# First loads in places of their own, and a wider margin behind TensorE's deferrable matmuls, in a planned hybrid-attention step

## Chip, core and metric

The kernel runs on one core of one Trainium2 chip. The metric is the device time of one execution in microseconds (us). The engines are TensorE (PE; its weight loads, PEld, run beside its matmuls), VectorE (DVE), ScalarE (ACT), GpSimd (POOL) and SyncE (SP), which issues the DMA transfers. TensorE's clock has two levels here, 2.4 and 1.2 GHz, and the profile gives the granted one as a share of the upper.

## What is computed

One layer of a streaming encoder, for 512 prompt rows and 32 sample rows of width 1024:

```python
z = _rmsnorm(x, g) @ w_in
qa, ka, va, ga, qb, kb, vb, gb, qm, gm, qi, ki, wi = _split_cols(z)
...
oa = _band_prompt(qa, ka, va, rel_bias_a[l])      # 6 heads: chunk band with a learned bias
ob = _dsa_prompt(qb, kb, vb, qi, ki, wi)          # 6 heads: keys chosen by an index score
om = _attend(qm, mk, mv, None)                    # 4 heads: 256 memory rows
xp = _merge(xp, oa, ob, om, ga, gb, gm, w_out)    # x + concat(o * silu(gate)) @ w_out
```

The sample rows do the same against caches of 1024 (or 512) past rows. For the second group an indexer of 8 heads by 32 scores every admissible key, `relu(qi . ki)` weighted by `wi`, and each query attends only to its best 128 (prompt) or 256 (sample) keys. The memory's keys and values are `_rmsnorm(mem) @ w_mem_kv`. Outputs are both results and the new cache rows.

## The kernel before

All 545 rows' projections are matmuls in three terms (high by high, low by high, high by low part), since TensorE takes rounded fp32 operands: `wh` and `wl` are the high and low part of a weight tile, `xTh` and `xTl` those of the transposed rows (tokens and samples beside each other, 544 columns). The order of the work is: the index projection, the keys' and values' projections (`ka`, `va`), memory keys and values (`mk`, `mv`), queries and gates (`EARLY`), then the second group (`LATE`), then the output projection. Attention, the index scores and the choice of keys are woven in between.

**The planner.** No order is written out by hand. The class `Line` (from L44) reckons a clock for every engine while the program is built: `cost` (L62) prices an instruction, `lag` (L87) the way from one engine to another, `had` (L121) says when a tile will be ready, `op` (L140) advances the clocks. The projections are the main thread (`run`, L204). Everything else is a task, a generator that yields the time at which it wants to go on; the tasks stand in a heap, and before every projection matmul `beside` (L191) runs the tasks that are due by then. Each engine gets its instructions in the order in which they are written, and takes them in that order on the chip. So a task's time decides how many projection matmuls stand in front of its own ones. That time is mostly `line.at(tiles)`, the reckoned readiness plus `margin`, 0.3 us (L169). `room` (L292) waits until the planner reckons a PSUM bank to be free.

**The weights.** `w_list` names all weight tiles in their order of use. `w_load` (L409) issues their loads into four buffers `raw` on SyncE's queue; a load waits until the tile four before it has been split and, where the sample rows use it too, used. `w_split` (L418) rounds `raw` to `wh` on ScalarE and subtracts to `wl` on GpSimd. `w_sample` (L445) multiplies the 32 sample rows with the unsplit `raw` (operand `xF`, eight matmuls a party, two for each `raw`; the trace has sixteen entries for the eight), and then itself moves the bank to SBUF on ScalarE, adds the four parts and scales them on VectorE. Parties are the index, the first and the second group's natural-order projections; the first four `raw` after the index's are the keys' (`ka`), the next four the values' (`va`).

**The first loads.** `START` (L36) is the order of the first loads: `x` is a part of the transposed rows, `w` a weight tile, `t` the rotary tables, `r` a tile of natural rows for the norms, `m` a half of the transposed memory. `rows_load` (L590) puts the prompt's and sample's rows into two alternating buffers `nat`, so a load waits for the norm of the rows two before; the memory's rows lie in the places of `rank` and `gate0`. `norms` (L604) squares and sums a tile of rows on ScalarE, and GpSimd makes its factor `rs`; `spread` (L618) turns `rs` into rows by TensorE. The memory norm's gain `g_mem` is loaded last in this run; `mTh`, the memory's high part, is made with it on ScalarE.

**The deferrable matmuls.** `index_prompt` (L798) and `index_sample` (L843) score keys by the index; `KSs` holds the sample's past index keys, of which VectorE subtracts the rounded part. `picks` finds the thresholds: for the sample by 22 tests, each of them `passed` (L936): ScalarE counts (`okf`, in the trace `bf_ok`), TensorE sums the counts in one matmul, VectorE sets the next threshold, so each test waits for the one before. `sample` (L1109) and `attend` (L1443) are the attention: scores, softmax (`z`, its sums `st`), transposes of `z` by `ident` into `pt`, and `pt` times values. `turned_pair` (L1279) transposes a head pair of `ka`.

Helpers record every operation on one line, so all rows of the trace show L233; the operand names tell them apart.

Of the kernel before, what the change touches and what calls it, by code (L numbers as in the profile page):

```python
# [9 lines left out]
F32 = mybir.dt.float32  # L10
# [3 lines left out]
ALU = mybir.AluOpType  # L14
# [3 lines left out]
P = 128  # L18
# [17 lines left out]
START = "wxwxwxwtwwrrrrwwrmmrr"  # L36
# [7 lines left out]
class Line:  # L44
# [41 lines left out]
    @staticmethod  # L86
    def lag(of, to):  # L87

        if of == to or of is None:
            return 0.127 if to == "DVE" else 0.09 if to == "POOL" else 0.0  # L90
        return 0.95 if of == "SP" else 0.26 if to == "PE" else 0.2 if of == "PE" else 0.06 if of == "POOL" else 0.15
# [77 lines left out]
    def at(self, *tiles):  # L169
        return max(self.had(x) for x in tiles) + self.margin  # L170

# [91 lines left out]
def hybrid_step(ctx: ExitStack, tc: tile.TileContext, a: dict):  # L263
# [28 lines left out]
    def room(k=1):  # L292

        yield from line.wait(lambda: len(free_banks) >= k)
        while True:
            t = sorted(pp.free(f"b{b}") for b in free_banks)[k - 1]
            if t <= line.now():
                return
            yield t
            yield from line.wait(lambda: len(free_banks) >= k)  # L300
# [10 lines left out]
    ka = cp.tile([P, NT, 384], F32, tag="ka", name="ka")  # L311
    va = cp.tile([P, NT, 384], F32, tag="va", name="va")
# [6 lines left out]
    ysS = cp.tile([P, PAST + T], F32, name="ysS")  # L319
# [89 lines left out]
    def w_load():  # L409
        party = {p + j for _, p, _ in parties for j in range(NK // 2)}  # L410
        for i, (w, k, nk, lo, hi) in enumerate(w_list):
            yield from line.wait(lambda: allowed[0] > i and len(split) > i - 4 and (i - 4 not in party or i - 4 in met))
            yield wp.free("raw")
            raw = wp.tile([P, nk, hi - lo], F32, tag="raw", name="raw", bufs=4)
            DMA.dma_start(raw, w[k * P:(k + nk) * P, lo:hi].rearrange("(k p) n -> p k n", p=P))
            raws.append(raw)
# [28 lines left out]
    def w_sample():  # L445
        for nm, i, n in parties:
            yield from line.wait(lambda: len(raws) > i + 1 and x_done[0] > 1)
            yield line.at(xF[:, 0:4, :], raws[i + 1])
            yield from room()
            p = bank()  # L450
            for j in (0, 2):
                yield from line.wait(lambda: len(raws) > i + j + 1 and x_done[0] > j + 1)
                yield line.at(raws[i + j], raws[i + j + 1], xF[:, 2 * j:2 * j + 4, :])
# [4 lines left out]
            yield line.at(p)  # L458
            if nm in ("kb", "vb"):
                yield from line.wait(lambda: 0 in over)  # L460
            out = (cp.tile([T, 384], F32, tag={"kb": "kaS", "vb": "vaS"}.get(nm, nm + "S"), name=nm + "S") if nm != "i"
                   else ix.tile([T, n], F32, name="zS"))
            A.copy(out, p[0:T, 0:n])
            for q in range(1, 4):
                yield line.at(out) - 0.2
                V.tensor_tensor(out, p[q * T:(q + 1) * T, 0:n], out, op=ALU.add)
            give(p)
            yield from line.wait(lambda: NT in normed)
            yield max(line.at(rs[0:T, NT:NT + 1]), line.at(out) - 0.2)
            V.tensor_scalar(out, out, rs[0:T, NT:NT + 1], None, op0=ALU.mult)  # L470
            news[nm] = out
            if nm in ("kb", "qb"):
                rope(out.rearrange("p (h d) -> p h d", d=64), out, T, 6, 64, ctab["cos64S"], ctab["sin64S"], V)
# [116 lines left out]
    def rows_load():  # L590
# [5 lines left out]
        if i <= NT:  # L596
            yield from line.wait(lambda: len(normed) > i - 2)
            t = rp.tile([P, D], F32, tag="nat", name="nat", bufs=2)
        else:
            t = cp.tile([P, D], F32, tag=("rank", "gate0")[i - NT - 1], name="nat")  # L600
# [17 lines left out]
    def spread():  # L618

        yield from line.wait(lambda: NT in normed)  # L620
        yield line.at(rs)
# [130 lines left out]
    def index():  # L752
        nonlocal ip, identR
        yield from line.wait(lambda: len(indexed) == NT and NT in normed)
        p1.close()
        ip = pool(ipx, "ip", "right")
        identR = ip.tile([P, P], F32R, name="identR")
        V.tensor_copy(identR, ident)
        for g in (index_sample(), index_prompt(), picks()):
            line.spawn(g)  # L760
        load_tables(64)
# [36 lines left out]
    def index_prompt():  # L798
# [5 lines left out]
        yield line.at(kst)  # L804
# [7 lines left out]
        for t in range(1, NT):  # L812
            n = P * (t + 1)
            yield line.at(qst[t])
# [11 lines left out]
            yield line.at(QS)  # L826
# [16 lines left out]
    def index_sample():  # L843
# [14 lines left out]
        yield line.at(qsS)  # L858
# [14 lines left out]
        yield line.at(kst2)  # L873
# [5 lines left out]
        for k0, n in ((0, 512), (512, 512), (1024, T)):  # L879
            yield line.at(KSs)  # L880
# [7 lines left out]
            yield line.at(*rs)  # L888
# [33 lines left out]
    def sample_choice():  # L922
# [13 lines left out]
        def passed(of, bias, least_, scale=1.0):  # L936
# [4 lines left out]
            yield line.at(okf) - 0.2  # L941
# [137 lines left out]
    natural = {"ka": ka, "va": va}  # L1079

    def projections(order):
        for nm in order:
# [17 lines left out]
            else:  # L1100
                if nm not in natural:

                    line.until(lambda: (2 if nm == "kb" else 0) in over)
                    natural[nm] = cp.tile([P, NT, 384], F32, tag=nm, name=nm)
                of = f"new_{nm[1]}_{nm[0]}"
# [3 lines left out]
    def sample(mix, nh, nb, kt, cv, qT, kn, vn, pts, zin):  # L1109
# [6 lines left out]
        if kn is not None:  # L1116
            yield line.at(kn)
# [7 lines left out]
        yield line.at(qT, *kt)  # L1125
        yield from room(3)
        o_ps = bank()
        for g0 in range(0, nh, 4):
# [35 lines left out]
            yield line.at(z)  # L1164
# [18 lines left out]
            yield line.at(*(x[0] for x in blocks))  # L1183
            yield line.at(*cv)
# [94 lines left out]
    def turned_pair(nat, hp, then):  # L1279

        w = nat.shape[1] * P
        yield line.at(nat[:, :, hp * P:(hp + 1) * P])
# [55 lines left out]
    class Masked:  # L1338
# [57 lines left out]
        def turn(self):  # L1396
            pts = []
            for e in range(2):
                yield from line.wait(lambda: places[self.w] > 0)
                places[self.w] -= 1  # L1400
                yield line.at(self.z[e])
# [41 lines left out]
    def attend(i):  # L1443
# [9 lines left out]
        yield line.at(*pair.q, *pair.k)  # L1453
# [12 lines left out]
        yield line.at(*pts)  # L1466
# [220 lines left out]
```

## Time and profile before

| | us |
|---|---|
| median of 3 runs | 384.17 |
| lowest, highest run | 383.58, 387.33 |
| the profiled execution | 385.51 |
| its span (first to last recorded instruction) | 383.7 |

The mean granted TensorE clock of the profiled execution is 0.984 of full speed. All rows come from that one execution, which took 1.34 us longer than the median; its span leaves 1.8 us of it before the first and behind the last instruction. A matmul's busy time in the rows is what it took at the granted clock, so a stretch at the lower clock looks busy and does half as much.

### The profile page before, as it was taken

What the parts mean: (1) busy time and instruction counts of PE and PEld (TensorE: products, weight loads), DVE (VectorE), ACT (ScalarE), POOL (GpSimd) and SP (SyncE); (2) the same over time, 40 slices, a digit from 0 to 9 for tenths busy, and PEclk for the clock granted to TensorE, in tenths of its full rate; (3) what the DMA queues carried; (4) which work ended last, traced back from release to release, by engine and by line L of the source; (5) the groups of instructions that cost most, each with busy time, mean ns of one, the idle gap of its engine ahead of it and who ended that gap; (6) DMA issues with size and microseconds to landing.
All of it is one profiled execution on the core that took longest, in us unless ns stands there. A gap on an engine that the chain in (4) does not pass through costs nothing.

```text
span 383.7 us, 7976 instructions
## 1 busy us (share of the span) xinstructions
PE 362.8 (95%) x2961; PEld 324.6 (85%) x2961; DVE 286.1 (75%) x721; ACT 224.5 (59%) x529; POOL 186.1 (49%) x199
## 2 busy tenths in 40 slices
PE   8997889999999999999898999799999999999992
PEld 8795768999989888898697888799999877999992
DVE  3664877988999999999999997787755587422453
ACT  5664946898677777756475674323654556411353
POOL 1778862377433665416668623735224310633552
PEclk9999989999999999999998999989999999999998
DMA  7969641156564422112401220522145940230005
GB/s 248 309 209 290 194 140 58 61 172 186 166 205 141 124 72 57 42 42 80 114 24 61 85 63 27 164 56 55 43 156 195 370 167 2 78 140 4 0 15 219
DMA packets 41478, 46.35 MB, mean 121 GB/s; under 512 B 5184, under 2 KB 36544, under 8 KB 41440
## 3 DMA queue, kind: packets, MB, share of 16 engines
q1 hardware_dynamic: 41440, 45.85, 38.0%
q8 instruction: 23, 0.38, 0.4%
q14 instruction: 15, 0.12, 0.1%
HBM read 39.67 MB, written 6.16 MB: 119 GB/s over the span
## 4 chain that ended last, share of the span: by engine, by line
PE 67%; DVE 21%; DMA 5%; ACT 3%; issue 2%; SPq 1%; POOL 1%; POOLq 0%; DVEq 0%; ACTq 0%
PE bank L233 67%; DVE ysel L233 3%; DVE m L233 2%; DMA g_mem<-in_norm_mem_g_dram 2%; DVE z L233 2%; DMA raw<-in_w_in_dram 2%; DVE rank L233 1%; DVE st L233 1%; DVE rt L233 1%; DVE qbS L233 1%; SPq L233 1%; DMA cbi<-in_cache_b_kidx_dram 1%; DVE kbS L233 1%; ACT sq L233 1%; DVE rot L233 1%
## 5 line engine op out<-in xcount | busy, mean ns | idle before, releaser
L233 POOL TENSOR_TENSOR wl<-raw,wh 128x512 fp32r<-128x512 f32 (+2 forms) x68 | 107.7, 1592 | 116.0 <-ACT wh L233 105.6
L233 ACT ACTIVATE wh<-raw 128x512 fp32r<-128x512 f32 (+2 forms) x70 | 49.5, 715 | 43.4 <-PE bank L233 18.1
L233 PE MATMUL bank<-wh,xTh 128*128 128x384 f32 (+1 forms) x192 | 67.9, 354 | 0.0
L233 PE MATMUL bank<-wl,xTh 128*128 128x384 f32 (+1 forms) x192 | 64.9, 338 | 1.8 <-POOL wl L233 1.7
L233 PE MATMUL bank<-wh,xTl 128*128 128x384 f32 (+1 forms) x192 | 64.7, 337 | 0.0
L233 ACT ACTIVATE z<-z,st 128x256 f32<-128x256 f32 (+3 forms) x73 | 39.0, 548 | 23.9 <-DVE st L233 23.9
L233 PE MATMUL bank<-xTh,wh 128*128 128x272 f32 x208 | 46.5, 304 | 0.4 <-DVE st L233 0.4
L233 PEld LDWEIGHTS bank<-wh,xTh 128*128 128x128 f32 x192 | 37.3, 194 | 7.4 <-issue 6.5
L233 PE MATMUL bank<-xTl,wh 128*128 128x272 f32 x208 | 43.0, 288 | 0.0
L233 PE MATMUL bank<-xTh,wl 128*128 128x272 f32 x208 | 42.9, 288 | 0.0
L233 PEld LDWEIGHTS bank<-wl,xTh 128*128 128x128 f32 x192 | 37.2, 194 | 2.6 <-POOL wl L233 2.2
L233 PEld LDWEIGHTS bank<-wh,xTl 128*128 128x128 f32 x192 | 37.3, 194 | 0.4 <-DVE xTl L233 0.3
L233 PEld LDWEIGHTS bank<-xTh,wh 128*128 128x128 f32 x208 | 32.6, 189 | 3.1 <-issue 1.8
L233 PEld LDWEIGHTS bank<-xTl,wh 128*128 128x128 f32 x208 | 32.6, 188 | 0.0
L233 PEld LDWEIGHTS bank<-xTh,wl 128*128 128x128 f32 x208 | 32.6, 189 | 0.0
L233 PE MATMUL bank<-ident,z 128*128 128x128 f32 (+1 forms) x161 | 26.0, 281 | 1.7 <-ACT pt L233 1.1
L233 DVE TENSOR_TENSOR xr<-bank,xr 128x256 f32<-128x256 f32 (+1 forms) x24 | 12.3, 512 | 19.8 <-PE bank L233 19.7
L233 DVE MAX8 m<-ysel 128x8 f32<-128x256 f32 (+2 forms) x48 | 26.3, 548 | 0.0
L233 DVE MATCH_REPLACE8 ysel<-m,ysel 128x256 f32<-128x256 f32 (+2 forms) x48 | 26.0, 543 | 0.0
L233 PEld LDWEIGHTS bank<-ident,z 128*128 128x128 f32 (+1 forms) x161 | 18.0, 142 | 5.8 <-issue 2.1
L233 ACT ACTIVATE junkS<-ysS,bi_neg 128x1056 int8<-128x1056 f32 x16 | 18.8, 1177 | 3.6 <-DVE bi_neg L233 3.6
L233 ACT COPY pt<-bank 128x512 f32<-128x512 f32 (+1 forms) x28 | 14.8, 539 | 8.8 <-PE bank L233 8.7
(308 smaller groups left out, 902.2 us busy)
## 6 DMA issues: line engine op xcount, KB each, us to landing
raw<-in_w_in_dram SPq DMA_DIRECT2D x20, 384.0 KB, 3.5
raw<-in_w_in_dram SPq DMA_DIRECT2D x26, 256.0 KB, 2.9
raw<-in_w_out_dram SPq DMA_DIRECT2D x8, 384.0 KB, 3.2
nat<-in_x_prompt_dram SPq DMA_DIRECT2D x4, 512.0 KB, 5.3
raw<-in_w_mem_kv_dram SPq DMA_DIRECT2D x8, 256.0 KB, 2.8
xr<-in_x_prompt_dram SPq DMA_DIRECT2D x4, 512.0 KB, 5.6
out_dram<-xr SPq DMA_DIRECT2D x4, 512.0 KB, 2.6
xr<-in_x_t_dram SPq DMA_DIRECT2D x3, 544.0 KB, 6.1
```

Of the source, the lines that this page charges most:

```text
L233: return fn(*args, **kw)
```

## The change

`START` puts all four keys' weights ahead of the rows, the four prompt and one sample row tiles behind them, and the memory rows behind the transposed memory. The first four of these `raw` tiles get places of their own (those of `q0` and `gate0`, which are written later), the next four then take the `raw` buffers, and none of the eight waits for a split. The rows 2 to 4 and the memory's get places of their own too (`ka`, `va`, `ysS`, `rank`, `gate0`), so that only the memory's wait, until the keys' samples are done with their weights. For that `ka`, `va` and `ysS` are allocated later. What follows the sample matmuls is a task of its own, `sample_rows`.

A new `Line.sure` reckons 1.0 us (`SURE`) behind the data instead of 0.3, and 20 places with a deferrable matmul use it instead of `at`; the choice's test, which took 0.2 off `at`, does too. `room` counts a bank as free 0.4 us later, and `lag` adds 0.3 us from a released place to TensorE.

```diff
-START = "wxwxwxwtwwrrrrwwrmmrr"
+START = "wxwxwxwtwwwwrrrrrmmrr"
+SURE = 1.0
...
+        if of is None and to == "PE":
+            return 0.3
         if of == to or of is None:
...
+    def sure(self, *tiles):
+
+        return max(self.had(x) for x in tiles) + SURE
...
-            t = sorted(pp.free(f"b{b}") for b in free_banks)[k - 1]
+            t = sorted(pp.free(f"b{b}") for b in free_banks)[k - 1] + 0.4
...
-    ka = cp.tile([P, NT, 384], F32, tag="ka", name="ka")
-    va = cp.tile([P, NT, 384], F32, tag="va", name="va")
+    ka = va = ysS = None
...
-            yield from line.wait(lambda: allowed[0] > i and len(split) > i - 4 and (i - 4 not in party or i - 4 in met))
-            yield wp.free("raw")
-            raw = wp.tile([P, nk, hi - lo], F32, tag="raw", name="raw", bufs=4)
+            yield from line.wait(lambda: allowed[0] > i and (i < 8 or len(split) > i - 4 and (i - 4 not in party or i - 4 in met)))
+            if i < 4:
+
+                if i % 2 == 0:
+                    first = cp.tile([P, 2, nk, hi - lo], F32, tag=("q0", "gate0")[i // 2], name="raw")
+                raw = first[:, i % 2]
+            else:
+                yield wp.free("raw")
+                raw = wp.tile([P, nk, hi - lo], F32, tag="raw", name="raw", bufs=4)
...
-                yield line.at(raws[i + j], raws[i + j + 1], xF[:, 2 * j:2 * j + 4, :])
+                yield line.sure(raws[i + j], raws[i + j + 1], xF[:, 2 * j:2 * j + 4, :])
...
+            line.spawn(sample_rows(nm, n, p))
+
+    def sample_rows(nm, n, p):
+        yield line.at(p)
...
-        if i <= NT:
-            yield from line.wait(lambda: len(normed) > i - 2)
+        if i < 2:
             t = rp.tile([P, D], F32, tag="nat", name="nat", bufs=2)
         else:
-            t = cp.tile([P, D], F32, tag=("rank", "gate0")[i - NT - 1], name="nat")
+            if i > NT + 1:
+                yield from line.wait(lambda: all(i in met for i in range(4)))
+            t = cp.tile([P, D], F32, tag=("ka", "va", "ysS", "rank", "gate0")[i - 2], name="nat")
...
-        yield from line.wait(lambda: len(indexed) == NT and NT in normed)
+        yield from line.wait(lambda: len(indexed) == NT and NT in normed and all(i in met for i in range(4)))
...
             for k0, n in ((0, 512), (512, 512), (1024, T)):
-            yield line.at(KSs)
+            yield line.sure(KSs)
             yield from room(2)
...
-            yield line.at(okf) - 0.2
+            yield line.sure(okf)
             yield from room()
...
-            yield line.at(z)
+            yield line.sure(z)
...
-                    line.until(lambda: (2 if nm == "kb" else 0) in over)
+                    line.until(lambda: NT - 1 in normed if nm[1] == "a" else (2 if nm == "kb" else 0) in over)
```

The first place is SyncE's queue behind the rotary tables, in the kernel before. `raw` 128x2x384 are the keys' and then the values' weights, `nat` natural rows, `mr` the transposed memory.

```order
L233 DMA raw<-in_w_in_dram 128x2x384 x2
L233 DMA nat<-in_x_prompt_dram 128x1024 x4
L233 DMA raw<-in_w_in_dram 128x2x384 x2
L233 DMA nat<-in_x_sample_dram 32x1024
L233 DMA mr<-in_mem_t_dram 128x4x256 x2
L233 DMA nat<-in_mem_prompt_dram 128x1024 x2
L233 DMA g_mem<-in_norm_mem_g_dram 128x8
```

The same place now:

```order
L240 DMA raw<-in_w_in_dram 128x2x384 x4
L240 DMA nat<-in_x_prompt_dram 128x1024 x4
L240 DMA nat<-in_x_sample_dram 32x1024
L240 DMA mr<-in_mem_t_dram 128x4x256 x2
L240 DMA nat<-in_mem_prompt_dram 128x1024 x2
L240 DMA g_mem<-in_norm_mem_g_dram 128x8
L240 DMA raw<-in_w_in_dram 128x2x384 x4
```

The third and fourth keys' weights moved ahead of four row tiles; the values' four weights, which stood seven issues further down, now follow the gain directly.

The second place is ScalarE after the first two index weights `wI` of the prompt, in the kernel before. `junk,ss` is a norm's square sum, `wh` a split.

```order
L233 ACTIVATE junk,ss<-nat 128x1024 x2
L233 ACTIVATE wh<-raw 128x768
L233 ACTIVATE junk,ss<-nat 32x1024
L233 ACTIVATE wh<-raw 128x768
L233 ACTIVATE stk<-rot 128x4x64
```

The same place now:

```order
L240 ACTIVATE junk,ss<-nat 128x1024 x2
L240 ACTIVATE mTh<-mr,g_mem 128x256
L240 ACTIVATE wh<-raw 128x768
L240 ACTIVATE junk,ss<-nat 32x1024
L240 ACTIVATE wh<-raw 128x768
```

A piece of the memory's high part moved ahead of the last keys' split and the sample's norm; the splits of the second and third keys' weights are no longer among these norms.

The third place is TensorE at the end of the index projection, now. `raw,xF` 32x384 are the keys' sample matmuls, which stood behind this projection, among the keys' own.

```order
L240 MATMUL bank<-wh,xTh_83 128x32
L240 MATMUL bank<-wh,xTl_85 128x32
L240 MATMUL bank<-wl,xTh_83 128x32
L240 MATMUL bank<-raw,xF 32x296 x4
L240 MATMUL bank<-raw,xF 32x384 x8
L240 MATMUL bank<-wh,xTh_83 128x296
L240 MATMUL bank<-wh,xTl_85 128x296
L240 MATMUL bank<-wl,xTh_83 128x296
```

The eight matmuls moved ahead of the projection's last quarter, so TensorE needs all four keys' weights before it.

The fourth place is TensorE in an attention piece over the memory, in the kernel before. `ident,z` transposes the softmax's `z`, `pt,mv` multiplies what came of it with the memory's values, `bf_ok,over` is a test of the choice.

```order
L233 MATMUL bank<-ident,z 128x128 x4
L233 LDWEIGHTS over_364
L233 MATMUL bank<-bf_ok,over_364 128x1
L233 MATMUL bank<-ident,mk 128x128 x2
L233 MATMUL bank<-ident,z 128x128 x4
L233 MATMUL bank<-pt,mv 64x128 x8
```

The same piece now, from the last of eighteen projection matmuls that follow `ident,mk`:

```order
L240 MATMUL bank<-wl,xTh_82 128x384
L240 MATMUL bank<-ident,z 128x128 x4
L240 MATMUL bank<-wh,xTh_82 128x384
L240 MATMUL bank<-wh,xTl_84 128x384
L240 MATMUL bank<-wl,xTh_82 128x384
L240 MATMUL bank<-wh,xTh_82 128x384
L240 MATMUL bank<-wh,xTl_84 128x384
L240 MATMUL bank<-wl,xTh_82 128x384
L240 MATMUL bank<-pt,mv 64x128 x8
```

Eighteen projection matmuls stand between the transposes of `mk` and those of `z`, and six between these and the product with the values, where none stood.

## Rows read from the trace of the kernel before

**Rows 1.** The page: busy us of each engine, share of the span, instructions.
```profile
PE 362.8 (95%) x2961; PEld 324.6 (85%) x2961; DVE 286.1 (75%) x721; ACT 224.5 (59%) x529; POOL 186.1 (49%) x199
```

**Rows 2.** Stretches: us, busy us (instructions) of PE, PEld, DVE, ACT, POOL, clock, DMA share, GB/s.
```profile
50.30:53.80 3.50, 3.50 (x16) 3.06 (x18) 3.47 (x4) 1.90 (x4) 3.25 (x4) 0.51 0.62 225
203.30:206.80 3.50, 3.04 (x22) 2.71 (x23) 3.37 (x9) 0.77 (x3) 3.05 (x4) 0.59 0.13 48
247.90:251.40 3.50, 3.36 (x12) 3.36 (x12) 3.09 (x4) 0.82 (x2) 2.21 (x1) 0.56 0.02 7
22.37:31.40 9.03, 9.03 (x52) 8.74 (x51) 4.63 (x14) 4.40 (x10) 7.43 (x20) 1.00 0.93 281
31.40:62.00 30.60, 26.14 (x161) 19.90 (x160) 21.53 (x35) 19.72 (x45) 20.24 (x30) 0.94 0.60 185
170.00:230.00 60.00, 55.96 (x459) 47.80 (x457) 57.63 (x131) 38.05 (x101) 35.90 (x32) 0.97 0.24 67
230.00:250.00 20.00, 17.61 (x121) 15.71 (x121) 15.43 (x29) 8.14 (x15) 11.30 (x9) 0.96 0.30 95
```

**Rows 3.** TensorE's waits, longest: matmul, releaser, total us, times, longest.
```profile
PE bank L233 <- ACT bf_ok L233: 2.4, 1, 2.4
...
PE bank L233 <- ACT z L233: 1.3, 1, 1.3
...
PE bank L233 <- DVE KSs L233: 1.1, 1, 1.1
...
PE bank L233 <- ACT pt L233: 1.1, 1, 1.1
...
PE bank L233 <- DVE pt L233: 0.8, 1, 0.8
...
PE bank L233 <- DVE ka L233: 0.7, 1, 0.7
```

**Rows 4.** Timeline of SyncE's queue: start, us on the queue, the DMA issued.
```profile
13.06 0.88 SPq L233 DMA_DIRECT2D raw<-in_w_in_dram  x2
13.99 9.52 SPq L233 DMA_DIRECT2D nat<-in_x_prompt_dram  x4
23.61 0.89 SPq L233 DMA_DIRECT2D raw<-in_w_in_dram  x2
```

**Rows 5.** DMA rate, 0 to 45 us in 40 slices of 1.125 us, from 0.
```profile
GB/s 0 11 273 303 322 318 294 390 380 387 350 153 63 337 378 386 405 62 22 0 211 288 255 378 381 252 211 312 353 403 408 311 216 150 204 69 136 395 388 393
```

**Rows 6.** Timeline of TensorE's matmuls: start, us, operation, in brackets idle us before, releaser.
```profile
32.56 0.45 PE L233 MATMUL bank<-wl,xTh 128*128 128x384 f32 x1 [1.12 <-POOL wl L233]
...
35.05 0.24 PE L233 MATMUL bank<-ident,rs 32*128 32x32 f32 x1 [1.08 <-POOL rs L233]
...
35.22 1.50 PE L233 MATMUL bank<-raw,xF 128*32 128x384 f32 x16
...
48.41 0.47 PE L233 MATMUL bank<-KSs,QSs 128*128 128x512 f32 x1 [1.14 <-DVE KSs L233]
```

**Rows 7.** Timeline of ScalarE, 31 to 33 us, columns as before.
```profile
31.14 1.06 ACT L233 ACTIVATE junk<-nat 32x1024 bf16<-32x1024 f32 x1 [1.84 <-DMA nat<-in_x_sample_dram]
32.20 0.83 ACT L233 ACTIVATE wh<-raw 128x768 fp32r<-128x768 f32 x1
```

**Rows 8.** Timelines of VectorE and of GpSimd from 45.3 us, columns as before.
```profile
45.46 2.80 DVE L233 TENSOR_TENSOR KSs<-cbi,KSs 64x1024 fp32r<-64x1024 f32 x1
...
45.34 1.84 POOL L233 TENSOR_TENSOR wl<-raw,wh 128x768 fp32r<-128x768 f32 x1 [1.02 <-ACT wh L233]
```

**Rows 9.** Views of tiles: count, ns (shortest, median, longest), first and last start, shapes.
```profile
L233 PE MATMUL bank<-bf_ok,over x22: 163/177/181, 69.3 to 248.0; 128*128 128x1 bf16 x22
...
L233 PE MATMUL bank<-keysB,qbS x36: 189/589/613, 306.7 to 323.0; 64*32 64x512 f32 x24, 64*32 64x32 f32 x12
...
L233 PEld LDWEIGHTS bank<-wh,oBh x48: 187/187/192, 357.6 to 375.6; 128*128 128x128 f32 x48
...
L233 ACT ACTIVATE oBh<-o x9: 292/311/420, 298.2 to 333.3; 128x128 fp32r<-128x128 f32 x6, 128x256 fp32r<-128x256 f32 x3
```

## Prediction made before the changed kernel was run

> **What bounds the kernel now.** I read the busy times first: TensorE is busy 362.8 us of a span of 383.7, so the time is TensorE's work plus the holes in it [rows 1]. Next the stretches: the holes lie in three places. From 31.40 to 62 us 4.46 us of 30.60 are idle, from 170 to 230 us 4.04 of 60, from 230 to 250 us 2.39 of 20 [rows 2]; together 10.9. The rest of the 20.9 idle us is the start, the tail behind the last matmul, and 1 us in small pieces. Third, the granted clock: 0.51, 0.59 and 0.56 over three stretches of 3.5 us [rows 2]. Each is a stretch at the lower level of 1.2 GHz, and what it costs is at most half of the busy time in it: about 1.7, 1.5 and 1.6, together 4.8. Fourth, TensorE's waits: the holes have names, each once: bf_ok 2.4, z 1.3, KSs 1.1, two of pt 1.1 and 0.8, ka 0.7 [rows 3], and in front wl 1.12 and rs 1.08 [rows 6]. TensorE takes its matmuls in the written order, so in each of these the matmul at the head was not ready while projection matmuls behind it were. No change of order can return more than 10.9 + 4.8 = 15.7 us.
>
> **The first loads.** The third and fourth of the keys' weights were behind four row loads, and these stood 9.52 us on SyncE's queue, because two of them wait for places [rows 4]. While SyncE waited the DMA engines ran dry: the rate falls to 63 GB/s at slice 12 and to 22 and 0 at slices 18 and 19 [rows 5]. That is why wl came 1.12 us late, and the sample's rows, which reached ScalarE at 31.14 [rows 7], made rs 1.08 late. Now nothing in that run of the queue waits for a place except the last memory rows, so both waits go: **-2.2 us**.
>
> What is late next? All loads now stand in one stream, and I time it by its bytes. It starts at 14.6 us, where slice 13 begins and the rate of the old kernel comes back. A full stream runs at 376 GB/s, the mean of slices 7 to 10 and of 13 to 16 alike; the mean of slices 20 to 33, with its gaps, is 295 [rows 5]. These are my two ends.
> - The keys' four weights, 1536 KB, have landed at 18.8 (19.9 at the low rate). The eight keys' sample matmuls, 1.50 us of work [rows 6], now stand ahead of the last quarter of the index projection. That quarter is 24 matmuls of 0.174 us at most (9.03 us for 52 [rows 2]) before 22.37, so TensorE comes to the last of these loads near 19: 0 to 0.9 us late.
> - The keys' projection then starts at 22.37 + 1.50 = 23.9. 66 of its matmuls at 0.174 bring TensorE to 35.4, where the first values' sample matmuls stand. Their second load is the 7524th KB of the stream: 35.1, or 40.7 at the low rate. Late by 0 to 5.3 us.
> - The memory norm's gain, a load of 4 KB, lies behind 5760 KB: 30.3 to 34.6. ScalarE now has mTh, which needs it, ahead of the fourth weights' split and of the sample's norm; so those two queue behind a load. In the old kernel 3.9 us passed from the sample rows' arrival, 31.14 [rows 7], to TensorE's release at 35.05 [rows 6]; with a split of 0.83 [rows 7] and mTh at as much again in front, TensorE is released at 35.9, or 40.2. It comes there at 35.4 + 0.75 (four sample matmuls) + 1.05 (six of the projection) = 37.2 at the earliest. Late by 0 to 3.0, and this hides behind the wait of the point above.
> - The rows are passed by 768 KB of weights but no longer wait for places: the first lands at 20.2, the fourth at 24.4, the sample's at 24.7, against 31.14 before. On ScalarE and GpSimd three splits of keys' weights now stand ahead of the first norm; nobody wants a norm before 37, so this costs nothing, nor does it that rows lie in the tiles of keys and values, which are first written after the keys' projection.
> I take 0.6 for all of it, near the fast end, since the full slices on both sides of each gap agree on 376; the ends are 0 and 5.3.
>
> **The margin.** A deferrable matmul was put 0.3 us behind its data as the planner reckons it, and is now put 1.0 behind; a bank's release 0 and now 0.4, with 0.3 more before TensorE is reckoned to start on it; the choice's test went from 0.1 to 1.0. Nothing is slept on the chip: the margin only sets how many projection matmuls stand in front. So each old wait shrinks by the added margin, at most to nothing: bf_ok 2.4 - 0.9 = 1.5, z 1.3 - 0.7 = 0.6, KSs 0.4, pt 0.7 (a bank) and 0.1, ka 0.3 (a bank). Of 7.4 remain 3.6: **-3.8 us**, with ends of 0 (as many waits at other places) and -7.4. At the memory units the order shows it: six projection matmuls now stand between z's transposes and pt's matmuls, where there were none.
>
> What else queues behind a later matmul? The longest serial chain is the sample's choice, 22 tests [rows 9]. At 0.9 us more each it ends 20 us later by plan, so its last test moves from 248.0 to about 268; the sample's scores begin at 306.7 [rows 9], so it stays hidden. At the end, the last attention piece leaves ScalarE at 333.3 and is first used at 357.6 [rows 9]; the new order has 152 matmuls behind its last attention piece, the old 213, so 24 us of cover become about 17. Both cost nothing.
>
> **The clock.** The falls came behind the largest holes: KSs, whose wait ends at 48.41 [rows 6], and ka right behind it, together 1.8; the two of pt, 1.9; bf_ok, 2.4. If the largest left is 1.5, I expect one fall of the three to stay: 4.8 - 1.6 = **-3.2 us**, with ends of 0 and -4.8.
>
> **Given back.** TensorE reaches the stage from 170 to 230 us some 4 us sooner, and there VectorE is busy 57.63 of 60 us [rows 2]: what it makes can hardly come sooner. The new order answers with more projection in front, but not everywhere: **+1.2**, ends 0 and 5.
>
> One measured pair bears on this. VectorE's subtraction of KSs took 2.80 us while GpSimd's wl ran from 45.34 for 1.84 [rows 8]; it ended 1.1 us after wl did, and that is what made TensorE wait 1.14. The Trainium skill has a rule for it (SBUF — State Buffer, section Who interferes with whom): GpSimd and VectorE share one pair of ports under an exclusive lock, and a VectorE instruction with two SBUF inputs waits out a GpSimd instruction that reads SBUF. The pair agrees with it. By that rule a margin of 1.0 does not cover a whole wl, and three such hits would leave 0.84 each, 2.5 us more, so that the sum would be 2.5 smaller; by the rows alone I count one, which is the 0.4 left of KSs.
>
> **Sum.** -2.2 + 0.6 - 3.8 - 3.2 + 1.2 = -7.4, with rounding of the small waits (three of 0.3 that fall wholly) -0.3: -7.7. The profiled execution took 385.51, so 377.8; the median of the runs is 1.3 below it, so **376.5** for the median.
>
> **Rivals.**
> 1. *VectorE is the bound from 60 to 230 us.* What the front saves is waited for again there: for it speak the 96% and that pt, z, KSs and ka are VectorE's or behind it; against it that projections remain to fill with. It takes back the 4 us of the front and one more fall of the clock: -7.7 + 4 + 1.7 = -2.0, 382.2.
> 2. *The order does not do what it says*: it is planned again from the first microsecond, so its waits are drawn anew and are as many. Then only the loads count, -1.6: 382.6. Against it: each wait had a neighbour that was ready.
> 3. *Slower: the load stream.* At 295 GB/s the values' weights come 5.3 us late to a matmul that now stands at TensorE's head, and the clock falls behind it, 1.7; the margin gains nothing, the old front waits are gone: 5.3 + 1.7 - 2.2 = +4.8, 389.0. It decides from a rate below some 305 GB/s. For it: the slices with gaps; against it: the gaps were SyncE's waits, which go.
> 4. *Everything goes*: neither waits nor falls are left, -2.2 - 7.4 - 4.8 - 0.9 = -15.3: 368.9.
>
> **How the numbers follow.** A measurement of this kernel can tell about 1% from no change, which is 380.3 to 388.0. Forecast (371 to 380.3) 0.62, rival 4 0.08, rival 1 0.16, rival 2 0.08, rival 3 0.06. The first two are faster: 0.70; rivals 1 and 2 and a little of the others are the same: 0.24; slower 0.06. The range leaves out half of rival 4 and most of rival 3: 370 to 383; the likeliest's own is 371 to 380.3.
>
> **What would show it.** Right: no gap in the GB/s of the first 38 us; no wait of wl or rs before 40 us; idle from 31 to 250 us down from 10.9 to about 5; one stretch at 1.2 GHz. Wrong: a wait for a load of raw near 35 us (rival 3); idle in the 170 to 230 stretch unchanged or larger with VectorE at 96% (rival 1); the same sum of waits under other names (rival 2).

## The result, and the profile of the changed kernel

The changed kernel took 380.97 us (median of 20 runs, 379.0 to 385.76) against 385.22 for the kernel before in the same runs: a ratio of 0.9888, 95% interval 0.9864 to 0.9912. That is 4.3 us less, where 7.7 less was forecast (376.5, from a median of 384.17): the direction was right, the size was not. The profiled execution took 382.36 us, 3.15 less than that of before.

TensorE's busy time and its share of the span hardly differ from [rows 1]. The page of the changed kernel:

```profile
PE 360.6 (95%) x2959; PEld 322.7 (85%) x2959; DVE 282.9 (74%) x732; ACT 221.4 (58%) x519; POOL 181.8 (48%) x196
```

By stretches (us, busy us and instructions of PE, PEld, DVE, ACT, POOL, clock, DMA share, GB/s), to be read beside [rows 2]. The last two are the stretches at the lower clock:

```profile
31.40:62.00 30.60, 29.43 (x175) 26.00 (x175) 22.18 (x41) 20.59 (x43) 20.86 (x27) 0.94 0.41 120
62.00:170.00 108.00, 106.38 (x911) 96.15 (x910) 95.98 (x301) 75.81 (x185) 48.28 (x49) 1.00 0.40 119
170.00:230.00 60.00, 57.31 (x460) 49.12 (x462) 54.96 (x132) 32.71 (x83) 33.53 (x31) 1.00 0.22 61
230.00:250.00 20.00, 15.91 (x110) 13.25 (x102) 17.65 (x29) 10.80 (x25) 11.49 (x7) 0.91 0.31 96
48.60:52.10 3.50, 3.50 (x17) 3.40 (x16) 2.15 (x3) 2.05 (x5) 1.34 (x1) 0.51 0.92 303
243.20:246.60 3.40, 2.96 (x10) 2.96 (x11) 2.25 (x8) 3.37 (x12) 0.81 (x1) 0.50 0.01 2
```

The kernel before, in the one of these stretches that [rows 2] does not have:

```profile
62.00:170.00 108.00, 107.55 (x916) 98.78 (x917) 99.87 (x312) 82.83 (x201) 51.75 (x47) 1.00 0.39 115
```

Idle time in the first of the stretches falls from 4.46 to 1.17 us and in the third from 4.04 to 2.69. From 62 to 170 us it rises from 0.45 to 1.62, and from 230 to 250 us from 2.39 to 4.09. Together 11.3 became 9.6. Two stretches at the lower clock are left of three; the third gone is worth some 1.7. The sum of both, 3.5, is about what the two profiled executions differ by.

TensorE's waits (total, times, longest), for [rows 3]:

```profile
PE bank L240 <- DVE o L240: 3.6, 1, 3.6
PE bank L240 <- DVE kb L240: 1.6, 1, 1.6
...
PE bank L240 <- DVE ka L240: 1.2, 1, 1.2
PE bank L240 <- POOL wl L240: 1.0, 2, 0.6
PE bank L240 <- ACT wh L240: 0.8, 1, 0.8
PE bank L240 <- DVE queried L240: 0.7, 1, 0.7
PE bank L240 <- ACT tg L240: 0.6, 1, 0.6
```

Every wait of [rows 3] but ka's is gone or below 0.5; ka's is 1.2 now, at another matmul. Others hold as much as those did: o, kb, ka, queried and tg make 7.7, where the six of before made 7.4 (the waits for weight splits, for rs and at the start are left out of both). Where does the longest come from? TensorE around it (start, us, operation, in brackets idle before and releaser):

```profile
239.71 0.34 PE L240 MATMUL bank<-wl,xTh 128*128 128x384 f32 x1
243.64 0.19 PE L240 MATMUL bank<-bf_ok,over 128*128 128x1 bf16 x1 [3.60 <-DVE o L240]
243.69 0.67 PE L240 MATMUL bank<-wh,xTh 128*128 128x384 f32 x1
```

The choice's test was ready long before (ScalarE wrote `bf_ok` at 235.87); what it lacked was a bank, which VectorE frees with `o`. VectorE and GpSimd ahead of that:

```profile
234.57 0.56 DVE L240 TENSOR_TENSOR qbS<-bank,qbS 32x384 f32<-32x384 f32 x1
235.16 1.98 DVE L240 TENSOR_SCALAR qbS<-qbS,rs 32x384 f32<-32x384 f32 x1
237.25 2.01 DVE L240 TENSOR_TENSOR rt<-qbS,sin64S 32x384 f32<-32x384 f32 x1
239.29 2.06 DVE L240 TENSOR_TENSOR qbS<-qbS,cos64S 32x384 f32<-32x384 f32 x1
241.39 0.55 DVE L240 TENSOR_TENSOR qbS<-rt,qbS 32x384 f32<-32x384 f32 x1
241.97 1.29 DVE L240 TENSOR_REDUCE st<-bank 128x2 f32<-128x512 f32 x2
243.17 0.41 DVE L240 SCALAR_TENSOR_TENSOR o<-bank,gate 128x256 f32<-128x256 f32 x1
```

```profile
233.13 2.03 POOL L240 TENSOR_TENSOR kb<-rt,kb 128x384 f32<-128x384 f32 x1 [1.43 <-DVE kb L240]
235.11 5.84 POOL L240 TENSOR_TENSOR wl<-raw,wh 128x768 fp32r<-128x768 f32 x3
```

GpSimd makes three low parts in a row, 5.84 us. In just that time three VectorE instructions on 32 rows by 384 take 2 us each. The fourth of the group, behind GpSimd's end, takes 0.55, and so does the first, which has an operand in PSUM and ran beside a GpSimd instruction. The three cost some 4.5 us more than alone (0.40, 0.55 and 0.55 in the runs below). That is enough for the wait of 3.60; the clock falls near its end, at 243.2.

The kernel before has the same. VectorE and GpSimd ahead of its wait of 2.4 us, which ends at 248.04:

```profile
239.35 1.06 DVE L233 TENSOR_SCALAR qbS<-qbS,rs 32x384 f32<-32x384 f32 x1
240.52 2.01 DVE L233 TENSOR_TENSOR rt<-qbS,sin64S 32x384 f32<-32x384 f32 x1
242.57 0.97 DVE L233 TENSOR_TENSOR qbS<-qbS,cos64S 32x384 f32<-32x384 f32 x1
243.58 2.08 DVE L233 TENSOR_TENSOR qbS<-rt,qbS 32x384 f32<-32x384 f32 x1
```

```profile
240.16 1.96 POOL L233 TENSOR_TENSOR wl<-raw,wh 128x768 fp32r<-128x768 f32 x1
242.09 1.05 POOL L233 TENSOR_TENSOR oMl<-o,oMh 128x256 fp32r<-128x256 f32 x1
243.10 2.15 POOL L233 TENSOR_TENSOR wl<-raw,wh 128x768 fp32r<-128x768 f32 x1
```

It is the same group of instructions. Two of them take 2 us behind low parts, and two take 0.4 and 0.7 longer than alone behind shorter GpSimd instructions (`oMl`, and a `kb<-rt,kb` from 239.19 for 1.02): some 4.1 us in all. The prediction had read this wait by its releaser (`bf_ok` of ScalarE) and looked no further back.

### The profile page after: what moved, and what is told of

It is laid out like the page before. It is cut to its first block, busy times and chain, and to the rows that moved or that the text cites. A ratio compares the mean times of both kernels' runs of the same rounds, so it can differ in the third digit from the quotient of the medians.

```text
span 380.6 us, 7964 instructions
## 1 busy us (share of the span) xinstructions
PE 360.6 (95%) x2959; PEld 322.7 (85%) x2959; DVE 282.9 (74%) x732; ACT 221.4 (58%) x519; POOL 181.8 (48%) x196
## 4 chain that ended last, share of the span: by engine, by line
PE 67%; DVE 21%; ACT 4%; issue 3%; POOL 2%; DMA 2%; SPq 1%; POOLq 0%; DVEq 0%; ACTq 0%
PE bank L240 67%; DVE ysel L240 5%; DVE m L240 2%; DVE rt L240 2%; DMA raw<-in_w_in_dram 2%; DVE qbS L240 2%; DVE rank L240 1%; POOL wl L240 1%; DVE st L240 1%; DVE kbS L240 1%; ACT sq L240 1%; ACT wh L240 1%; DVE junkS L240 1%; POOL ss L240 1%; ACT junkS L240 1%
## 5 line engine op out<-in xcount | busy, mean ns | idle before, releaser
L240 ACT ACTIVATE z<-z,st 128x256 f32<-128x256 f32 (+3 forms) x70 | 38.0, 557 | 27.0 <-DVE st L240 26.8
L240 PE MATMUL bank<-ident,z 128*128 128x128 f32 (+1 forms) x161 | 25.2, 275 | 0.6 <-ACT tg L240 0.6
L240 DVE SCALAR_TENSOR_TENSOR ysel<-r,wI,ysel 128x256 f32<-128x256 f32 (+2 forms) x21 | 18.9, 898 | 4.5 <-ACT r L240 3.7
```

Source lines behind the costliest of these rows:

```text
L240: return fn(*args, **kw)
```

## The experiments

The theory (A): TensorE's large waits are made by VectorE instructions that wait out a GpSimd instruction, which the planner does not know; a margin covers them only by chance. The rivals: (B) every new order draws its waits anew, and no part has a gain of its own; (C) the gain is the loads' alone. Ratios are to the kernel before in the same runs; 0.01 is 3.85 us.

**One part alone.** `loads_only` puts the margins back (the first diff); `margin_only` puts the loads back (START, the second diff, with the places, allocations and sample code of before):

```diff
-SURE = 1.0
+SURE = 0.3
...
-        if of is None and to == "PE":
-            return 0.3
...
-            t = sorted(pp.free(f"b{b}") for b in free_banks)[k - 1] + 0.4
+            t = sorted(pp.free(f"b{b}") for b in free_banks)[k - 1]
...
-            yield line.sure(okf)
+            yield line.at(okf) - 0.2
```

```diff
-START = "wxwxwxwtwwwwrrrrrmmrr"
+START = "wxwxwxwtwwrrrrwwrmmrr"
```

> The changed kernel with the margins of the old one (0.3, the choice's test at 0.1, banks at 0, no 0.3 from a released place); the loads, their places and sample_rows stay. Theory A (the loads' gain is real; what the margin does is undone because VectorE's instructions on SBUF wait out GpSimd's, which the planner doesn't know): wl and rs no longer wait before 40 us, so 1.5 to 2.5 us less than before, ratio 0.993 to 0.996, and the big waits of 2 us and more stay behind 60 us. Theory B (every new order draws its waits anew, neither part has a gain of its own): anything from 0.985 to 1.005, with large waits at other places than in either kernel. Theory C (the whole gain is the loads'): 0.987 to 0.990.

> The old kernel's loads with the changed kernel's margins. Theory A: the waits of wl and rs, 2.2 us, are back in front; of the waits behind 40 us those stay that follow a VectorE instruction stretched by GpSimd; 0.994 to 1.0 of before. Theory C: 1.0. If the margin is worth what was forecast for it (3.8 us and two falls of the clock): 0.983 or less.

Measured: 0.9839 (0.9796 to 0.9882) for the loads alone, 6.2 us; 0.9941 (0.9914 to 0.9969) for the margin alone, 2.3 us. For the loads that is more than A and C gave them, and just beyond the fast end of B. For the margin it is the edge of what A gave: wl's wait in front is 2.4 there, and behind 40 us the waits of [rows 3] are gone from their places, but ka, qbS, gate and z hold 1.0, 1.1, 1.0 and 0.9 at others. The stretch of the front in `loads_only`, and what became of `KSs` there (its VectorE instruction, then the matmuls that use it):

```profile
31.40:62.00 30.60, 30.34 (x188) 25.67 (x186) 20.69 (x38) 20.74 (x45) 21.20 (x33) 1.00 0.43 119
```

```profile
L238 DVE TENSOR_TENSOR KSs<-cbi,KSs x1: 2291/2291/2291, 49.3 to 49.3; 64x1024 fp32r<-64x1024 f32 x1
```

```profile
52.12 0.34 PE L238 MATMUL bank<-wl,xTh 128*128 128x384 f32 x1
52.30 0.62 PE L238 MATMUL bank<-KSs,QSs 128*128 128x512 f32 x2
```

The idle 4.46 us of the front are 0.26, and the fall of the clock at 50.3 is gone with them. `KSs` is still stretched (2.29 against 1.22 alone), but it is done at 51.6 and TensorE comes to it at 52.3 with projection in front. So the loads removed not only wl's and rs's waits but those of KSs and ka, and their fall, too. Behind the front `loads_only` has one fall of the clock, about twice as long as the others, at a wait for kb:

```profile
225.97 0.64 PE L238 MATMUL bank<-wh,xTh 128*128 128x384 f32 x1 [1.77 <-DVE kb L238]
```

```profile
226.00:232.60 6.60, 5.94 (x18) 5.40 (x18) 5.52 (x14) 3.44 (x12) 2.09 (x3) 0.50 0.01 4
```

The two parts alone sum to 8.5 us and together give 4.3: something of 4 us came in only with both.

**The one collision taken out of the changed kernel.** The three low parts of 235 to 241 us are made without GpSimd's reads, all orders kept. First by ScalarE (`nc.scalar.activation(wl, raw, AF.Copy)` in `wl_by_act`), then, since that moved other work, by a fill on GpSimd (`wl_zero`):

```diff
-            tsub(V if i in WV else G, wl, raw, f(wh))
+            if i in (48, 49, 50):
+                line.op("POOL", "tensor_tensor", [wl], [raw, f(wh)], {})
+                nc.gpsimd.memset(f(wl), 0.0)
+            else:
+                tsub(V if i in WV else G, wl, raw, f(wh))
```

> The changed kernel, all engines in the same order, but the three low parts that GpSimd makes from 235 to 241 us are written by ScalarE, which is idle there, as plain copies of raw (so the low parts of one weight group are not what they should be). Theory A: qbS's three VectorE instructions take 0.4 to 0.55 us instead of 2.0, the wait of 3.6 us falls below 0.5, the fall of the clock at 243 us goes with it: 4 to 5.5 us less than the changed kernel, ratio to before 0.975 to 0.979. Theory B or a VectorE that is late for other reasons: the wait stays at 2 us or more, ratio 0.985 to 0.990.

> As wl_by_act, but GpSimd fills the three low parts with zeros (it writes and reads nothing; the low parts of one weight group are left out), so ScalarE's queue and TensorE's order are those of the changed kernel. Theory A: qbS's instructions take 0.4 to 0.55 us, the choice's wait of 3.6 us falls below 0.6, the waits of pt stay at 0.4 and 0.1, where the copies on ScalarE had made them 1.3 and 0.8; 3.5 to 5.5 us less than the changed kernel, ratio to before 0.975 to 0.980. If VectorE is late for its own work: the wait stays above 2 us and the ratio at 0.985 to 0.990.

Measured: `wl_by_act` 0.9853 (0.9794 to 0.9911), a miss. The choice's wait was gone and qbS's instructions took 0.41 to 0.55, but the copies stood on ScalarE ahead of `pt`, whose waits grew from 0.4 and 0.1 to 1.3 and 0.8, and the clock fell there for nearly 7 us, at most 3.3 us of time:

```profile
233.60:240.40 6.80, 6.72 (x38) 6.16 (x39) 2.81 (x5) 3.85 (x13) 0.73 (x1) 0.52 0.85 264
```

`wl_zero` gave 0.9781 (0.9749 to 0.9812), 8.4 us less than before and 4.1 less than the changed kernel. Its VectorE, GpSimd and TensorE at the place:

```profile
234.06 2.23 DVE L240 TENSOR_SCALAR qbS<-qbS,rs 32x384 f32<-32x384 f32 x1
236.40 0.55 DVE L240 TENSOR_TENSOR rt<-qbS,sin64S 32x384 f32<-32x384 f32 x1
236.98 0.55 DVE L240 TENSOR_TENSOR qbS<-qbS,cos64S 32x384 f32<-32x384 f32 x1
237.56 0.55 DVE L240 TENSOR_TENSOR qbS<-rt,qbS 32x384 f32<-32x384 f32 x1
```

```profile
233.99 2.09 POOL L446 MEMSET wl<- 128x768 f32 x3
```

```profile
239.81 0.18 PE L240 MATMUL bank<-bf_ok,over 128*128 128x1 bf16 x1 [0.88 <-DVE o L240]
```

The wait fell from 3.60 to 0.88 and the clock no longer falls behind it. It did not fall below 0.6 as expected, because one of the three instructions, the scaling, was held up by the fills as well (2.23 for 0.40). The idle time from 230 to 250 us fell by 2.4 and the fall at 243 us was worth at most 1.5: together 3.9 of the 4.1. The other fall, at 48.6 us, is absent from this profile too, at a place that the edit does not touch (ka still waits 1.49 there). With this collision out, the change is worth about the sum of its parts.

**The same test on the kernel before.** Fills in place of three of its low parts, in its own order:

```diff
+            if i in (8, 48, 49):
+                line.op("POOL", "tensor_tensor", [wl], [raw, f(wh)], {})
+                nc.gpsimd.memset(f(wl), 0.0)
```

> The kernel before, all engines in its order, but GpSimd fills three low parts with zeros instead of subtracting (one at 45.34 us, two between 240 and 246 us; the low parts of those weight tiles are left out). If its waits of KSs, ka and the choice (1.1, 0.7, 2.4) were made by VectorE instructions that waited out GpSimd's: all three below 0.4, the falls of the clock behind them (50.3 and 248.3) gone, 5 to 7.5 us less, ratio 0.981 to 0.987. If the planner's reckoning was short by small amounts everywhere, as the prediction had it: the waits shrink by less than half, ratio 0.991 or more.

Measured: 0.9873 (0.9835 to 0.9911), 4.9 us, just short of what was expected. `KSs` is back to 1.22 us, though it starts beside the end of a fill (VectorE, then GpSimd):

```profile
44.79 1.22 DVE L233 TENSOR_TENSOR KSs<-cbi,KSs 64x1024 fp32r<-64x1024 f32 x1
```

```profile
44.37 0.74 POOL L435 MEMSET wl<- 128x768 f32 x1
```

The waits of KSs and ka are gone, the choice's is 0.4, and both falls behind them are gone. A wait for z at 215 us, which the kernel before did not have, is 1.8, with a fall at its side: part of the gain was given back there. So three of the six waits from which the prediction subtracted its margin were made by stretched instructions. The other three, z and the two of pt, no run takes apart.

**The planner taught.** One thing more in the planner's reckoning, added to the changed kernel (`lock_plan`), to the one before (`before_lock`), and to each part alone (`loads_lock`, `margin_lock`):

```diff
+    def locks(op, outs, ins, kw):
+        if any(x.space == PSUM for x in outs + ins):
+            return False
+        if op == "tensor_scalar":
+            return outs[0].dtype == F32 and ins[0].dtype == F32 and "accum_out" not in kw and outs[0].free_size() > 1
+        return op in ("tensor_tensor", "scalar_tensor_tensor", "tensor_tensor_reduce")
...
+        if eng == "DVE" and self.locks(op, outs, ins, kw):
+            for s, e in self.held:
+                if s <= t < e - 0.15:
+                    t = e - 0.15
...
+            if eng == "POOL" and ins and d > 0.3:
+                self.held.append((t, end))
```

> The changed kernel with one thing more in the planner: a VectorE instruction that works on SBUF alone with two tensors, or scales fp32 there, and would start while a GpSimd instruction runs is reckoned to start 0.15 us before that one ends. Theory A: no wait above 1.2 us is left behind 40 us that follows a stretched instruction, idle from 31 to 250 us falls from 8.4 to about 4, at most one fall of the clock: ratio to before 0.973 to 0.982. Theory B: other waits take their place, 0.985 to 0.992.

> The kernel before with nothing new but the planner's knowledge of the stretched VectorE instructions. Theory A: KSs's and the choice's waits (1.1 and 2.4) and their falls of the clock go, the loads' waits in front (wl and rs, 2.2) stay: 4 to 7 us less, ratio 0.982 to 0.990. If the knowledge helps only where the margin is wide: 0.994 to 1.0.

> The loads and the planner's knowledge, with the old margins. If the wide margin is worth something once stretched instructions are reckoned: slower than lock_plan by 1.5 us and more, ratio 0.977 to 0.985. If the margin only stood in for that knowledge: within 1 us of lock_plan, 0.970 to 0.976.

> The old loads with the margins and the planner's knowledge: the fourth corner beside before_lock (0.981), margin_only (0.994) and lock_plan (0.973). The loads' own waits in front, about 2 us and a fall of the clock at most, are what is missing against lock_plan: 0.977 to 0.984.

| loads | margin | planner as it was | planner taught |
|---|---|---|---|
| old | old | 1 | 0.9809 (0.9776 to 0.9842) |
| new | old | 0.9839 (0.9796 to 0.9882) | 0.9903 (0.9871 to 0.9935) |
| old | new | 0.9941 (0.9914 to 0.9969) | 0.9820 (0.9772 to 0.9868) |
| new | new | 0.9888 (0.9864 to 0.9912) | 0.9731 (0.9682 to 0.9780) |

`lock_plan` is the fastest kernel of the study, 10.4 us below before. Its stretches:

```profile
31.40:62.00 30.60, 30.60 (x191) 27.30 (x190) 20.53 (x38) 20.56 (x44) 21.55 (x27) 1.00 0.46 131
62.00:170.00 108.00, 107.05 (x934) 97.04 (x933) 95.89 (x303) 79.03 (x192) 53.38 (x54) 1.00 0.41 116
170.00:250.00 80.00, 76.50 (x584) 66.26 (x583) 73.30 (x171) 46.45 (x115) 43.09 (x36) 1.00 0.26 73
```

4.5 us are idle from 31 to 250 us where the changed kernel had 9.6, and the clock does not fall in this execution, the second fastest of six: its mean granted clock is 0.993, that of the others 0.987 to 0.991. The knowledge alone, in the kernel before, gives 7.4 us: more than the whole change. `loads_lock` was a miss in a direction that none of the theories had: its largest wait is of another kind.

```profile
227.28 0.66 PE L254 MATMUL bank<-wh,xTh 128*128 128x384 f32 x1 [4.08 <-DVE kb L254]
```

Here a projection itself waits for a bank that VectorE frees by kb's rotation, and no VectorE instruction in the 10 us before is stretched; instructions of the prompt's choice, sums of the softmax and the sample's additions stand ahead. The changed kernel's wait of 1.6 for kb is of this kind too. It is not one of the matmuls that the margin is put on; in `lock_plan` the longest wait for kb is 0.7.

The parts do not add up in the last column either. With the taught planner the wide margin gains 0.017 with the new loads and nothing with the old; the new loads lose 0.009 with the old margin and gain 0.009 with the wide one (there the two intervals still overlap). So A names the cause of the waits it was tested on, and beside it a new order still draws other waits, as B says.

**Small steps.** Two kernels change SURE alone, 0.9 and 2.0; two more do so with the taught planner, 0.9 and 1.4:

```diff
-SURE = 1.0
+SURE = 0.9
```

> The changed kernel with SURE at 0.9 instead of 1.0, a step far too small to be worth anything as a margin: it only makes the planner write another order. If collisions of VectorE with GpSimd fall where they fall (each order draws its own): the time differs from the changed kernel's 0.9888 by 0.3% and more, most likely downward, 0.977 to 0.987, and the wait of 3.6 us is not there or is of another size. If the changed kernel's waits are a property of the margin's size: 0.987 to 0.991 with the same wait in front of the choice's test.

> The changed kernel with SURE at 2.0: a margin wider than the longest stretch seen (a whole wl, 1.84 less 0.15 us). Theory A with one stretch in front of a wait: waits above 1 us behind 40 us vanish except where several stretches follow each other, ratio 0.975 to 0.983. Theory B (orders draw their waits anew): 0.983 to 0.993, with waits of 1.5 us and more at new places. If later data hurt (banks held longer, VectorE with less to do ahead): above 0.993.

> The same step of 0.1 for the planner that reckons stretched VectorE instructions. If that knowledge takes the chance out: 0.970 to 0.977, as with 1.0 (0.9731). If 0.9731 was one lucky order: 0.979 or more.

> That planner with SURE at 1.4. The stretched instructions are reckoned, so more margin has little left to cover: 0.970 to 0.978. If the margin itself still pays: 0.968 or less. If wide margins cost (banks held longer, VectorE's work bunched): 0.979 or more.

Measured: 0.9846 (0.9797 to 0.9895) and 0.9826 (0.9785 to 0.9868) untaught, 0.9747 (0.9701 to 0.9794) and 0.9754 (0.9703 to 0.9806) taught. The intervals of 0.9, 1.0 and 2.0 do not part cleanly, but the waits do: with 0.9 the longest wait in front of a test of the choice is 1.5, and the longest of all is elsewhere. With 2.0 the longest is 1.9, at a product with the memory's values. The longest of all with 0.9:

```profile
201.94 0.44 PE L240 MATMUL bank<-wh,xTh 128*128 128x384 f32 x1 [3.13 <-DVE oSt L240]
```

Untaught, a step of 0.1 moves the large wait to another place (B's mechanism), and it is again one behind stretched instructions (A's cause in part: 2.15 us of stretch in the 10 us before a wait of 3.13). Taught, three neighbours agree within 0.0023. Not all of their waits are gone: with 1.4 one of 3.2 us is left, behind 3.8 us of stretch that fell otherwise than reckoned. Nor are all falls of the clock: the profile of 0.9 has one of some 7 us from 223 us on, that of 1.4 three.

**A second profile.**

> The changed kernel once more, for a second profile. If the wait of 3.6 us in front of the choice's test belongs to the order: it is there again, 3 to 4 us, with qbS's instructions at about 2 us. The wait of ka at 47.5 us and the fall of the clock behind it were there in one of two kernels with the same front and not in another, so either may come.

Measured: the wait is there again, 3.6 us, with qbS's instructions at 1.97, 2.01 and 2.07; ka's wait was 0.9 with its fall. The profile shown above is no accident of one execution.

## Why the prediction came out wrong

**The first loads: right in kind, too small.** That wl's and rs's waits go was right. The keys' weights and the rows no longer wait on the queue, and the stream is full up to slice 27 but for a dip at slices 20 and 21, [rows 4] and [rows 5] in the changed kernel:

```profile
10.68 3.57 SPq L240 DMA_DIRECT2D raw<-in_w_in_dram  x4
14.32 1.88 SPq L240 DMA_DIRECT2D nat<-in_x_prompt_dram  x4
...
24.40 11.13 SPq L240 DMA_DIRECT2D raw<-in_w_in_dram  x4
```

```profile
GB/s 0 13 226 355 262 270 355 381 393 402 364 274 312 373 374 409 385 397 411 400 280 245 332 354 403 393 364 372 299 83 28 0 137 325 248 234 188 242 51 0
```

From slice 13 to 27 the mean is 366 GB/s, near the fast end that was chosen. Then the queue does wait: the last of the values' four weights is issued at 35.17 only, and the rate falls to 83, 28 and 0 GB/s in slices 29 to 31. So the sign "no gap in the GB/s of the first 38 us" did not come, but the gap cost nothing: no matmul from 24 to 40 us waits for a load, and the values' second weights landed at 33.88 and were first used at 35.89. Rival 3 did not happen. Its 5.3 was too much even at its own rate: by the order of the loads those weights end with the 6532nd KB of the stream, not the 7524th, which at 295 GB/s is 37.3 and 1.9 late. (The places of `q0` and `gate0` hold the index's four weights, and it is for the index's sample matmuls that the memory rows wait, not for the keys'.) The term of -1.6 measured -6.2: KSs's and ka's waits and their fall of the clock (1.1 + 0.7 + 1.7 = 3.5), booked under the margin and the clock, go with the loads alone, and with the 2.2 of wl and rs make 5.7 (in the changed kernel ka's wait is back, with its fall). Which of the two edits, the order or the places, brings that was not tried apart.

**The margin: the step that failed.** "So each old wait shrinks by the added margin, at most to nothing", hence 3.6 of 7.4 left: -3.8. Alone the margin gave 2.3 us with all that hangs on it, and in the changed kernel 7.7 us of such waits are left. The premise, that the planner is short by small amounts everywhere, was wrong where most time lay. For three of the six old waits and for the longest new one it was short by whole GpSimd instructions where VectorE meets them, and a new order meets them elsewhere: 4.5 us of stretch on one chain gave the wait of 3.6. The prediction had the price of a hit on the table and counted one, by the rows alone. What came is the sign of rival 2, the same sum of waits under other names (7.4, now 7.7); only that rival's price of the loads, -1.6, does not hold.

The Trainium skill's rule was weighed there (SBUF — State Buffer, section Who interferes with whom), and three hits were taken as 0.84 each, 2.5 in all, left by a margin of 1.0. By the Trainium skill a scaling in a two-port mode, or a product with two inputs in SBUF, waits until a GpSimd instruction that reads SBUF is done. The trace agrees: one scaling and two products take 1.98, 2.01 and 2.06 beside low parts of 5.84 in all. But they came behind one another, and the margin is subtracted once, not three times.

**The clock.** One fall was forecast to stay, two stayed: -1.7 instead of -3.2. That falls follow the largest waits held in part: behind 3.60 and 1.17 there is one each, and the profiles of `wl_zero` and `lock_plan` have none. But kb's 1.57 has none, ka's 1.49 in `wl_zero` has none, and in `before_zero` the two of pt have none, 1.06 and 0.83 as large as in the kernel before, where a fall stood at them. Falls also differ between executions of one kernel: over the changed kernel's 20 runs the mean granted clock lies between 0.979 and 0.992, of which one fall of 3.4 us makes some 0.0045 (an estimate: half of 3.4 in 380.6). A count of falls is that of one execution.

**Given back.** 1.2 was taken for VectorE's own lateness; kb's wait of 1.57 without any stretch is of that kind, at about that size. Rival 1 was right in kind for this one place: VectorE is busy 54.96 of the 60 us.

**The sum.** -7.7 was forecast, -8.4 is what the change gives with that one collision taken out, -4.3 with it. The closeness of the first two is partly luck: the loads were too small by 4.6, and the rest, -6.1, was too large by 3.8 (-2.3 alone). Two small terms were off as well: three waits of 0.3 that fall wholly are 0.9, as in rival 4, not 0.3, and waits of that size are still there; and the median lies 0.3 below the profiled execution over 20 runs, not 1.3.

## What to carry to other kernels

Read a wait two links back: not only who released it, but whether the instructions ahead of the releaser took longer than the same ones do elsewhere in the trace. A margin is for many small errors of a plan; where the plan lacks one large, known cost, put the cost into the plan (here 0.9888 became 0.9731 by it, though 0.9839 became 0.9903 with the loads alone). When an order is planned anew, price the collisions that the new order may meet, one behind another, not only the waits that the old one had.

## What the runs showed of the hardware

VectorE instructions that work on SBUF alone with two tensors, or scale fp32 there, are held until a GpSimd instruction that is running and reads SBUF ends. They take their own time plus what is left of the other, less some 0.15 us: `KSs` 1.22 became 2.80 with 1.72 us of a low part left as it started, a product of `qbS` 0.55 became 2.01 with 1.60 left, its scaling 0.40 became 1.98 with 1.77 left. Instructions with an operand in PSUM are not held (`qbS<-bank` 0.56 beside one). It goes both ways: GpSimd's `kb<-rt,kb`, 1.02 alone, took 2.03 when it started beside a VectorE instruction of 1.31.

Fills on GpSimd read nothing. Not expected was that they hold the fp32 scaling up through three of them (2.23 for 0.40). They do not hold a product with two tensors: in `before_zero` `KSs` started with 0.32 us of a fill left and took its own 1.22, and a product of `qbS` with 0.24 left took its own 0.55. Held, they would have taken 1.39 and 0.64 by the sum above; no product started earlier in a fill. The Trainium skill has both cases (SBUF — State Buffer, section Who interferes with whom): a copy or scaling in a two-port mode shuts GpSimd out or is shut out by it, a product with two inputs in SBUF meets only a GpSimd instruction that reads. The first agrees with the 2.23, the second with the 2.80 beside a low part and the 1.22 beside a fill.
